# Product 3 of two feature tiles of gate and up computed in Strassen's form

## The chip, the cores and the metric

One Trainium2 chip; the program runs on one of its cores. The metric is the device time of one execution in microseconds. A core has TensorE (PE, matmuls, with its weight loads shown as PEld), VectorE (DVE), ScalarE (ACT), GpSimd (POOL) and SyncE (SP, which here issues the DMA transfers). Each engine works its own instructions in order; waits on semaphores join them.

## The reference

One inference step of a hybrid decoder layer with a model width of 1024, on 16 meta tokens, 1024 prompt tokens and 8 sample tokens, 1048 in all. The part that matters here is the feed-forward block, which stands before and after the mixer, with 2816 features:

```
def swiglu(x, wg, wu, wd):
    return (jax.nn.silu(x @ wg) * (x @ wu)) @ wd
...
h = h + 0.5 * swiglu(rmsnorm(h, n1), w1g, w1u, w1d)
...
h = h + 0.5 * swiglu(rmsnorm(h, n2), w2g, w2u, w2d)
```

Everything is float32. Here `x @ wg` and `x @ wu` are called gate and up.

## The kernel before

Features lie in 22 tiles of 128. For one tile, gate and up are computed together as a 2 x 2 block product: the left side has gate and up as its rows and the two halves of the 1024-long contraction (four K tiles of 128 each) as its columns; the right side has the two K halves as rows and two token parts as columns. A block of the right side exists for each of two token halves c; the token quarters are 262 wide in the first FFN and 258 in the second. The 2 x 2 product is done in Strassen's form (Winograd's variant), with seven products in place of eight, numbered 1 to 7, from sums of weight blocks (left) and sums of token blocks (right).

Float32 accuracy comes from splitting each operand into a high part (a float32r copy) and a low part (the difference), and three matmuls for each K tile: high with high, high with low, low with high (`mm3`, L163 to L165). So one product is 2 token halves x 4 K tiles x 3 = 24 matmuls and one tile is 7 x 24 = 168.

The products run in the order 1, 6, 2, 5, 7, 3, 4. Each writes a pair of PSUM banks ("acc", two pairs in rotation); 2 adds to the pair that 1 has filled, 3 to that of 5, and 4 to that of 7. When both token halves of a product are done, VectorE or ScalarE reads the pair (`post` in `pair`): ScalarE copies 1 (L574); VectorE adds 6 (L576), multiplies 2 by the norm's factor (L569) and ScalarE takes silu of it (L581), VectorE adds 5 (L583), 7 (L585), 3 (L587) and 4 (L593), and multiplies silu(gate) by up into the hidden tile (L608). All of TensorE, VectorE, ScalarE and SP is issued in an order written out by hand: `Steps` holds a list of half products (12 matmuls each, 14 for one feature tile), and every other job is put before the step with a given number.

For the left side (`Left`, from L465 on) the weights are loaded eleven steps before the tile's first product (L476, 256 KB each: gate and up, two K halves), the four sums stand seven to five steps before it on VectorE (L482), and the splits run just ahead of the products: ScalarE casts (L486), VectorE subtracts (L490). The right side's split operands are made once per FFN by `Blocks` and stay.

The hidden tiles of two feature tiles at a time go through `Hidden.jobs`: VectorE makes four differences (L734), and SP stores seven blocks to DRAM (L737), from where the down product loads them later. The slots that matter: 9 temporaries "t" of 524 columns, 8 raw weight tiles "r", 6 split weight tiles "ws", 8 slots "s" and 30 slots "u" of 1056 columns; in PSUM four banks "acc" and four banks "mis".

In the first FFN the first two feature tiles are done without Strassen's form (`Plain`); in the second FFN the first two go through `pair` in a special order. The other twenty tiles of each FFN go through `pair` one by one, with `Hidden.jobs` behind every two.

Of the kernel before, what the change touches and what calls it, by code (L numbers as in the profile page):

```python
# [9 lines left out]
F32 = mybir.dt.float32  # L10
# [326 lines left out]
class Blocks:  # L337
# [25 lines left out]
    def src(self, p):  # L363

        return self.b[7 if p == 12 else p]
# [74 lines left out]
class Steps:  # L440
# [9 lines left out]
    def add(self, mm, post=None):  # L450
        self.steps.append((mm, post))

    def run(self):
        for i, (mm, post) in enumerate(self.steps):
            for fn in self.at.pop(i, ()):
                fn()
            mm()
            if post:
                post()
        for i in sorted(self.at):  # L460
            for fn in self.at[i]:
                fn()


class Left:  # L465
# [27 lines left out]
        self.hi(p)  # L493
        self.lo(p)

    def plan(self, S, s0, late, sums):
        for ps, ds, fn in (
            ((1, 7, 4, 2), (-11, -11, -10, -10), self.load),
            ((5, 6, 7, 3), [d + sums for d in (-7, -7, -6, -5)], self.sum_),
            (ORDER, [2 * i - 4 + late for i in range(7)], self.hi),  # L500
            (ORDER, [2 * i - 3 + late for i in range(7)], self.lo),
        ):
            for p, d in zip(ps, ds):
                S.before(s0 + d, lambda p=p, fn=fn: fn(p))
# [195 lines left out]
            S.before(at + i, lambda fn=fn, n=n: fn(n))  # L700


FP = DFF // P // 2

DORDER = (1, 5, 6, 7, 3, 4, 2)
# [3 lines left out]
class Hidden:  # L709
# [3 lines left out]
        self.K = K  # L713
        self.d = {p: K.dram.tile([P, 2, FP, self.K.Q], F32, name=K.uid("hd")) for p in ORDER}

    def jobs(self, S, i, hid, e0, e1):

        K = self.K
        t, b = {}, {}

        def block(n):

            return hid[n // 2][0][:, n % 2 * 2 * self.K.Q : n % 2 * 2 * self.K.Q + 2 * self.K.Q]

        def val(p):
            return b[p] if p in b else block({1: 0, 12: 1, 2: 2, 3: 3}[p])

        def sub(p, x, y):
            s = {5: 0, 6: 0, 7: 1, 4: 1}[p]
            if s not in t:  # L730
                t[s] = K.slot("s", self.K.T)
            o = (p in (6, 4)) * 2 * self.K.Q
            b[p] = t[s][:, o : o + 2 * self.K.Q]
            K.nc.vector.tensor_sub(b[p], val(x), val(y))  # L734

        def store(p):
            K.nc.sync.dma_start(self.d[p][:, :, i, :], halves(val(p)))  # L737

        ks = (1, 3, 5) if i < FP - 1 else (1, 2, 3)
        for at, args in zip((e0 + 1, *(e1 + k for k in ks)), ((5, 12, 1), (6, 3, 5), (7, 3, 12), (4, 2, 6))):  # L740
            S.before(at, lambda args=args: sub(*args))
            S.before(at + 2, lambda p=args[0]: store(p))
        for at, p in ((e0 + 2, 1), (e1 + 1, 3), (e1 + 2, 2)):
            S.before(at, lambda p=p: store(p))

    def load(self, S, p, at):
# [148 lines left out]
def ffn(K, wg, wu, wd, ops, spread, src, first, after, late_r, plain=False):  # L895
# [10 lines left out]
    with K.tc.manual_schedule(engines={E.PE, E.DVE, E.Activation, E.SP}):  # L906
# [3 lines left out]
        if plain:  # L910
            hid = [[], []]
            lefts = [Left(K, [w[:, k : k + 4, f * P : f * P + P] for w, k in ((wgv, 0), (wuv, 0), (wuv, 4), (wgv, 4))], 4) for f in range(2)]
            first(S, *lefts)
            for f in range(2):
                p = Plain(K, lefts[f], ops, spread, hid[f], f == 1)
                p.add(S)
                p.late(S, late_r + 6 * f)
            hidden.jobs(S, 0, hid, late_r + 6, late_r + 12)
        for i in range(int(plain), NF // 2):
            hid, e = [], []  # L920
            for f in (2 * i, 2 * i + 1):
                hid.append([])
                pair(K, S, wgv, wuv, f, ops, spread, hid[-1], late_r, f == (2 if plain else 1), first if f == 0 else None)
                e.append(len(S.steps))
            hidden.jobs(S, i, hid, *([late_r + 6, max(late_r + 7, e[1])] if i == 0 else e))
# [1355 lines left out]
```

## Time and profile before

| | |
|---|---|
| runs | 1946.50, 1946.09, 1944.43 us; median 1946.09 |
| span of the profiled execution | 1943.5 us |
| PE busy | 99% |
| DVE busy | 74% |
| ACT busy | 42% |
| POOL busy | 5% |
| matmuls | 16,800 |
| DMA | 258 MB, 133 GB/s mean |

The page gives the span of one profiled execution, from its first to its last instruction, and beside it the busy share of each engine. Matmuls are pipelined: a row shows one as 0.28 to 0.29 us long, though the next one starts 0.12 us after it. So what TensorE does is read from the starts of its matmuls and from the waits in brackets, not from its busy share. A row of the timeline gives the start, the duration, the engine, the line, the operation, and in brackets how long the engine had been idle and what released it. The page gives no time around the span; the profiled execution stands 2.6 us under the median of the runs.

The steady part of gate and up lies at about 110 to 340 us (first FFN) and 1300 to 1620 us (second FFN).

### The profile page before, as it was taken

The page shows a single profiled execution, that of the slowest core. Times are in us where ns is not written, and L with a number is a line of the kernel's source. Part 1 is how long each engine was busy: PE and PEld are TensorE (multiplying, and loading weights), DVE is VectorE, ACT ScalarE, POOL GpSimd, SP SyncE. Part 2 cuts the span into 40 slices and gives each one's busy share as a digit, 9 for nine tenths or more (in the row PEclk, how much of TensorE's full clock was granted, in tenths as well). Part 3 has the DMA queues.
Part 4 walks back from the last instruction along what each step waited for, and adds up shares of the span by engine and source line. Part 5 has one row for each costly group of instructions (what it writes and reads, how often), then busy time and mean ns, then how long its engine had stood idle before and what let it go on. Part 6 is the DMA issues. An engine that isn't in the chain of part 4 may idle for free.

```text
span 1943.5 us, 41139 instructions
## 1 busy us (share of the span) xinstructions
PE 1921.7 (99%) x16800; PEld 1887.7 (97%) x16800; DVE 1434.7 (74%) x2516; ACT 823.6 (42%) x1558; POOL 90.3 (5%) x144
## 2 busy tenths in 40 slices
PE   9999999999999999999999999999999999999998
PEld 8999999999999999999899999999999999999998
DVE  7877777778688877576575556987777777768974
ACT  7522222224543644466564545742222222354343
POOL 3000000000000510000000002200000000000000
PEclk9999999999999999999999999999999999999999
DMA  8142332325977541221453254223332433487852
GB/s 246 47 129 83 101 114 83 114 85 157 289 230 257 172 146 53 64 88 48 117 160 93 79 176 137 91 80 99 94 104 82 124 90 100 153 257 231 280 182 86
DMA packets 324207, 258.45 MB, mean 133 GB/s; under 512 B 18923, under 2 KB 298731, under 8 KB 324011
## 3 DMA queue, kind: packets, MB, share of 16 engines
q1 hardware_dynamic: 323779, 255.79, 43.4%
q8 instruction: 132, 2.16, 0.4%
q14 instruction: 56, 0.46, 0.1%
q0 software_dynamic: 224, 0.04, 0.0%
q10 hardware_dynamic: 16, 0.00, 0.0%
HBM read 190.79 MB, written 65.05 MB: 132 GB/s over the span
## 4 chain that ended last, share of the span: by engine, by line
PE 93%; DVE 4%; issue 1%; ACT 1%; DMA 1%; SPq 0%; POOL 0%; DVEq 0%; ACTq 0%; POOLq 0%
PE acc L163 29%; PE acc L164 28%; PE acc L165 28%; PE mis L1677 1%; PE mis L1390 0%; DVE u L376 0%; PE mis L1739 0%; PE mis L1384 0%; DMA s<-in_x_prompt_dram 0%; DVE ws L490 0%; DVE t L321 0%; PE mis L1768 0%; PE mis L1377 0%; PE mis L1668 0%; PE mis L223 0%
## 5 line engine op out<-in xcount | busy, mean ns | idle before, releaser
L163 PE MATMUL acc<-u,ws 128*128 128x258 f32 (+3 forms) x4514 | 1316.4, 292 | 5.6 <-DVE t L583 2.3
L165 PE MATMUL acc<-u,ws 128*128 128x258 f32 (+3 forms) x4514 | 1304.0, 289 | 1.3 <-DVE ws L490 1.3
L164 PE MATMUL acc<-u,ws 128*128 128x258 f32 (+3 forms) x4514 | 1304.8, 289 | 0.2 <-DVE u L324 0.2
L163 PEld LDWEIGHTS acc<-u,ws 128*128 128x128 f32 x4514 | 852.6, 189 | 15.3 <-issue 10.0
L164 PEld LDWEIGHTS acc<-u,ws 128*128 128x128 f32 x4514 | 854.9, 189 | 1.4 <-DVE u L324 0.7
L165 PEld LDWEIGHTS acc<-u,ws 128*128 128x128 f32 x4514 | 852.2, 189 | 2.6 <-DVE ws L490 2.1
L490 DVE TENSOR_TENSOR ws<-r,ws 128x512 fp32r<-128x512 f32 x302 | 208.4, 691 | 69.6 <-ACT ws L486 69.5
L486 ACT CAST ws<-r 128x512 fp32r<-128x512 f32 x302 | 170.3, 614 | 4.8 <-DVE r L482 4.8
L602 ACT ACTIVATE t<-t 128x516 f32<-128x516 f32 (+1 forms) x43 | 27.4, 640 | 289.3 <-DVE t L569 289.3
L482 DVE TENSOR_TENSOR r<-r,r 128x512 f32<-128x512 f32 x168 | 115.7, 690 | 8.4 <-DMA r<-in_w_ffn_up_dram 6.8
L581 ACT ACTIVATE t<-t 128x516 f32<-128x516 f32 (+1 forms) x41 | 26.2, 639 | 197.2 <-DVE t L569 197.2
L762 DVE TENSOR_TENSOR u<-u,u 128x1048 fp32r<-128x1048 f32 (+3 forms) x84 | 97.2, 1158 | 9.8 <-ACT u L758 9.8
L250 POOL TENSOR_TENSOR t<-t,t 128x262 f32<-128x262 f32 (+1 forms) x56 | 58.2, 1048 | 783.2 <-DMA u<-hd 601.3
L158 DVE TENSOR_TENSOR ws<-r,ws 128x512 fp32r<-128x512 f32 x88 | 60.9, 700 | 40.6 <-ACT ws L157 40.1
L569 DVE TENSOR_TENSOR t<-t,u 128x516 f32<-128x516 f32 (+1 forms) x127 | 85.1, 697 | 2.8
L758 ACT CAST u<-u 128x1048 fp32r<-128x1048 f32 (+3 forms) x84 | 83.0, 988 | 4.0 <-DMA u<-hd 4.0
L820 ACT CAST ws<-u 128x512 fp32r<-128x512 f32 (+1 forms) x72 | 42.1, 585 | 98.9 <-DVE u L815 96.8
L825 DVE TENSOR_TENSOR ws<-r,ws 128x512 fp32r<-128x512 f32 (+1 forms) x84 | 56.3, 679 | 29.4 <-ACT ws L820 29.4
L849 DVE SCALAR_TENSOR_TENSOR s<-acc,s 128x524 f32<-128x524 f32 (+3 forms) x86 | 53.8, 649 | 32.8 <-PE acc L165 32.5
L820 ACT CAST ws<-r 128x512 fp32r<-128x512 f32 (+1 forms) x84 | 48.0, 582 | 65.1 <-DVE r L815 30.2
L574 ACT COPY t<-acc 128x516 f32<-128x516 f32 (+2 forms) x43 | 25.0, 582 | 103.5 <-PE acc L165 102.5
L569 DVE TENSOR_TENSOR t<-acc,u 128x516 f32<-128x516 f32 (+1 forms) x41 | 28.7, 699 | 49.5 <-PE acc L165 49.5
(420 smaller groups left out, 1844.8 us busy)
## 6 DMA issues: line engine op xcount, KB each, us to landing
r<-in_w_ffn_down_dram SPq DMA_DIRECT2D x128, 256.0 KB
hd<-s SPq DMA_DIRECT2D x93, 258.0 KB
r<-in_w_ffn_gate_dram SPq DMA_DIRECT2D x88, 256.0 KB
r<-in_w_ffn_up_dram SPq DMA_DIRECT2D x88, 256.0 KB
hd<-s SPq DMA_DIRECT2D x77, 262.0 KB
u<-hd SPq DMA_DIRECT2D x36, 516.0 KB
u<-hd SPq DMA_DIRECT2D x28, 524.0 KB
r<-in_w_in_dram SPq DMA_DIRECT2D x56, 256.0 KB
```

Source lines behind the costliest of these rows:

```text
L158: self.nc.vector.tensor_sub(lo, src, hi.bitcast(F32))
L163: mm(ps, whi, xhi, start=first, stop=False, skip_group_check=more)
L164: mm(ps, whi, xlo, start=False, stop=False, skip_group_check=more)
L165: mm(ps, wlo, xhi, start=False, stop=last, skip_group_check=more)
L250: K.nc.gpsimd.tensor_add(self.sq[q], self.sq[q], t)
L482: self.K.nc.vector.tensor_tensor(self.raw[p], self.raw[x], self.raw[y], op)
L486: self.K.nc.scalar.copy(self.w[p][:, : self.n * P], self.raw[p])
L490: self.K.nc.vector.tensor_sub(t[:, 512 : 512 + w], self.raw[p], t[:, :w].bitcast(F32))
L569: nc.vector.tensor_mul(t, t if src is None else src, spread.lanes(i, cs))
L758: K.nc.scalar.copy(hi, lo.bitcast(F32))
L762: K.nc.vector.tensor_sub(lo, lo.bitcast(F32), hi.bitcast(F32))
L820: nc.scalar.copy(w[p, j, g][:, : n * P], src)
```

## The change

In both FFNs, twenty of the feature tiles are taken two at a time (`two_pairs`, ten calls for each FFN). The two tiles still run products 1, 6, 2, 5, 7, 4 one after the other, each in 2 token halves: 12 steps for one tile in place of 14. Product 3 of the two tiles is taken out of them and done as one 2 x 2 block product of its own, again in Strassen's form: its rows are the two feature tiles, its contraction halves are two K tiles each, its columns are the two token quarters c. That is seven sub-products of 2 K tiles x 3 = 6 matmuls (`Third`). They run inside the second tile, one behind each of its steps 3 to 9 (`Steps.also`), in the order 1, 6, 2, 7, 5, 3, 4, into single banks "mis", 262 or 258 columns wide.

The left sums of the sub-products are made on VectorE from the raw weight sums of product 3 (`Third.sums`, four subtractions or additions 256 wide), and split by ScalarE and VectorE (`Third.hi`, `Third.lo`: three 512 wide, one 256 wide). Their results are combined by ScalarE (two copies) and VectorE (five additions 262 or 258 wide, `Third.post`) into a slot "s", and `second` adds them to the gate of the second token quarters of each tile (on VectorE, 524 or 516 wide; before, `post` of product 3 added its PSUM sum there). The right operands of the sub-products are sums of token blocks; `SubBlocks` makes them once for each FFN, behind the first two feature tiles: twelve VectorE instructions and four ScalarE casts 524 or 516 wide, kept in three slots "s" and one slot "u".

`Left` still loads the same weights eleven steps ahead and makes the same four sums. The seven stores of `Hidden.jobs` stay; that of block 1 is put nine steps earlier (`first=-7`).

```
--- before.py
+++ after.py
@@ -450,6 +450,11 @@
     def add(self, mm, post=None):
         self.steps.append((mm, post))
+    def also(self, fn):
+        mm, post = self.steps[-1]
+        self.steps[-1] = (mm, lambda: (post and post(), fn()))
     def run(self):
         for i, (mm, post) in enumerate(self.steps):
             for fn in self.at.pop(i, ()):
@@ -493,12 +498,12 @@
         self.hi(p)
         self.lo(p)
-    def plan(self, S, s0, late, sums):
+    def plan(self, S, s0, late, sums, order=ORDER):
         for ps, ds, fn in (
             ((1, 7, 4, 2), (-11, -11, -10, -10), self.load),
             ((5, 6, 7, 3), [d + sums for d in (-7, -7, -6, -5)], self.sum_),
-            (ORDER, [2 * i - 4 + late for i in range(7)], self.hi),
-            (ORDER, [2 * i - 3 + late for i in range(7)], self.lo),
+            (order, [2 * i - 4 + late for i in range(7)], self.hi),
+            (order, [2 * i - 3 + late for i in range(7)], self.lo),
         ):
             for p, d in zip(ps, ds):
                 S.before(s0 + d, lambda p=p, fn=fn: fn(p))
@@ -700,6 +705,232 @@
             S.before(at + i, lambda fn=fn, n=n: fn(n))
+ORDER2 = (1, 6, 2, 5, 7, 4)
+SUB = (1, 6, 2, 7, 5, 3, 4)
+class SubBlocks:
+    def __init__(self, K, ops):
+        self.K, self.ops = K, ops
+    def jobs(self, S, at):
+        K = self.K
+        nc = K.nc
+        b, hi, lo = {}, {}, {}
+        w = 2 * K.Q
+        def part(t, a):
+            return t[:, a * w : a * w + w]
+        def join(n, a, c):
+            b[n] = K.t(w)
+            h, l = self.ops[c].op[3]
+            nc.vector.tensor_add(b[n], part(h, a).bitcast(F32), part(l, a).bitcast(F32))
+        def sub(n, x, y):
+            nc.vector.tensor_sub(b[n], b[x], b[y])
+        def place(n):
+            s, i = {6: (0, 0), 7: (0, 1), 5: (1, 0), 4: (1, 1)}[n]
+            for d, tags in ((hi, "su"), (lo, "ss")):
+                if s not in d:
+                    d[s] = K.slot(tags[s], 2 * w, F32R)
+            self.op[n] = part(hi[s], i), part(lo[s], i)
+        names = {5: 11, 7: 12, 6: 22, 4: 21}
+        def cast(n):
+            place(n)
+            nc.scalar.copy(self.op[n][0], b[names[n]])
+        def low(n):
+            nc.vector.tensor_sub(self.op[n][1], b[names[n]], self.op[n][0].bitcast(F32))
+        self.op = {}
+        todo = [
+            [(join, 11, 0, 0), (join, 12, 0, 1)],
+            [(sub, 11, 12, 11), (join, 22, 1, 1)],
+            [(sub, 12, 22, 12), (sub, 22, 22, 11), (cast, 6)],
+            [(low, 6), (cast, 7), (join, 21, 1, 0)],
+            [(low, 7), (sub, 21, 21, 22), (cast, 5)],
+            [(low, 5), (cast, 4)],
+            [(low, 4)],
+        ]
+        for i, fns in enumerate(todo):
+            for fn, *args in fns:
+                S.before(at + i, lambda fn=fn, args=args: fn(*args))
+    def right(self, m):
+        if m in self.op:
+            return self.op[m]
+        a, c = {1: (0, 0), 2: (1, 0), 3: (1, 1)}[m]
+        w = 2 * self.K.Q
+        return tuple(t[:, a * w : a * w + w] for t in self.ops[c].op[3])
+class Third:
+    def __init__(self, K, lefts, sub):
+        self.K, self.lefts, self.sub = K, lefts, sub
+        self.w, self.ps = {}, {}
+    def plan(self, S, s1):
+        for d, fn, *args in (
+            (-2, self.sums, 0),
+            (-1, self.sums, 1),
+            (0, self.hi, 0),
+            (1, self.lo, 0),
+            (1, self.hi, 1),
+            (2, self.lo, 1),
+            (2, self.sums, 2),
+            (3, self.hi, 2),
+            (4, self.lo, 2),
+            (5, self.hi, 3),
+            (6, self.lo, 3),
+        ):
+            S.before(s1 + d, lambda fn=fn, args=args: fn(*args))
+    def sums(self, i):
+        x, y = (l.raw[3] for l in self.lefts)
+        sub, add = self.K.nc.vector.tensor_sub, self.K.nc.vector.tensor_add
+        h0, h1 = slice(0, 2 * P), slice(2 * P, 4 * P)
+        if i == 0:
+            self.r = self.K.raw()
+            sub(self.r[:, h0], x[:, h0], y[:, h0])
+            add(y[:, h0], y[:, h0], y[:, h1])
+        elif i == 1:
+            sub(self.r[:, h1], y[:, h0], x[:, h0])
+        else:
+            sub(x[:, h1], x[:, h1], self.r[:, h1])
+    def src(self, i):
+        x, y = (l.raw[3] for l in self.lefts)
+        return {0: x, 1: self.r, 2: y, 3: x[:, 2 * P :]}[i]
+    def hi(self, i):
+        src = self.src(i)
+        self.w[i] = self.K.ws()
+        self.K.nc.scalar.copy(self.w[i][:, : src.shape[1]], src)
+    def lo(self, i):
+        src, t = self.src(i), self.w[i]
+        w = src.shape[1]
+        self.K.nc.vector.tensor_sub(t[:, 512 : 512 + w], src, t[:, :w].bitcast(F32))
+    def mm(self, m):
+        K = self.K
+        t, o = {1: (0, 0), 2: (0, 256), 7: (1, 0), 6: (1, 256), 5: (2, 0), 4: (2, 256), 3: (3, 0)}[m]
+        b = {2: 1, 3: 5, 4: 7}.get(m, m)
+        if b not in self.ps:
+            self.ps[b] = K.psm()[:, : K.Q]
+        x = self.sub.right(m)
+        for k in range(2):
+            ks = slice(k * K.Q, k * K.Q + K.Q)
+            wh, wl = (self.w[t][:, d + o + k * P : d + o + k * P + P] for d in (0, 512))
+            K.mm3(self.ps[b], wh, wl, x[0][:, ks], x[1][:, ks], m == b and k == 0, k == 1, m != b)
+    def post(self, m):
+        K = self.K
+        nc, ps = K.nc, self.ps
+        if m == 1:
+            self.v = halves(K.t(2 * K.Q))
+            nc.scalar.copy(self.v[:, 0], ps[1])
+        elif m == 6:
+            nc.vector.tensor_add(self.v[:, 0], ps[6], self.v[:, 0])
+        elif m == 2:
+            q = K.slot("s", 4 * K.Q)
+            self.q = [halves(q[:, f * 2 * K.Q : f * 2 * K.Q + 2 * K.Q]) for f in range(2)]
+            nc.scalar.copy(self.q[0][:, 0], ps[1])
+        elif m == 5:
+            nc.vector.tensor_add(self.v[:, 1], ps[5], self.v[:, 0])
+            nc.vector.tensor_add(self.q[1][:, 1], ps[7], self.v[:, 1])
+        elif m == 3:
+            nc.vector.tensor_add(self.q[0][:, 1], ps[5], self.v[:, 0])
+        elif m == 4:
+            nc.vector.tensor_add(self.q[1][:, 0], ps[7], self.v[:, 0])
+def two_pairs(K, S, wg, wu, i, ops, spread, hids, sub, tight):
+    nc = K.nc
+    cs = slice(0, 2)
+    s0 = len(S.steps)
+    s1 = s0 + 2 * len(ORDER2)
+    tm = [{}, {}]
+    lefts = []
+    for n in range(2):
+        fs = slice((2 * i + n) * P, (2 * i + n) * P + P)
+        lefts.append(Left(K, [wg[:, 0:4, fs], wu[:, 0:4, fs], wu[:, 4:8, fs], wg[:, 4:8, fs]], 4))
+        lefts[n].plan(S, (s0, s1)[n], int(tight and n == 0), (3, 2)[n] * int(tight), ORDER2)
+    third = Third(K, lefts, sub)
+    third.plan(S, s1)
+    def temp(f, n):
+        if n not in tm[f]:
+            tm[f][n] = halves(K.t(2 * K.Q))
+        return tm[f][n]
+    def gate(f, n, t, src):
+        nc.vector.tensor_mul(t, src, spread.lanes(n, cs))
+        nc.scalar.activation(t, t, AF.Silu)
+    def out(f, n, u):
+        nc.vector.tensor_mul(u, u, spread.lanes(n, cs))
+        if not hids[f]:
+            hids[f].append(K.slot("s", K.T))
+        nc.vector.tensor_mul(halves(hids[f][0][:, n * 2 * K.Q : n * 2 * K.Q + 2 * K.Q]), temp(f, f"g{n}"), u)
+    def post(f, p, b):
+        if p == 1:
+            nc.scalar.copy(temp(f, "v"), b)
+        elif p == 6:
+            nc.vector.tensor_add(temp(f, "v"), b, temp(f, "v"))
+        elif p == 2:
+            gate(f, 0, temp(f, "g0"), b)
+        elif p == 5:
+            nc.vector.tensor_add(temp(f, "g1"), b, temp(f, "v"))
+        elif p == 7:
+            nc.vector.tensor_add(temp(f, "u1"), b, temp(f, "g1"))
+        elif p == 4:
+            u = temp(f, "v")
+            nc.vector.tensor_add(u, b, u)
+            out(f, 0, u)
+    def second(f):
+        g = temp(f, "g1")
+        nc.vector.tensor_add(g, g, third.q[f])
+        gate(f, 1, g, g)
+    def third_step(m):
+        third.mm(m)
+        third.post(m)
+    for f in range(2):
+        unit = Unit(K, lefts[f].w, [o.op for o in ops], 4, lambda p, cs, b, f=f: post(f, p, b))
+        for p in ORDER2:
+            for c in range(2):
+                j = len(S.steps) - s1
+                unit.step(S, p, c, (0, 1))
+                if 3 <= j < 10:
+                    S.also(lambda m=SUB[j - 3]: third_step(m))
+    S.before(s1 + 9, lambda: second(0))
+    S.before(s1 + 10, lambda: out(0, 1, temp(0, "u1")))
+    S.before(s1 + 11, lambda: second(1))
+    S.before(s1 + 12, lambda: out(1, 1, temp(1, "u1")))
+    return s1 + 10, s1 + 12, -7
 FP = DFF // P // 2
 DORDER = (1, 5, 6, 7, 3, 4, 2)
@@ -713,7 +944,7 @@
         self.K = K
         self.d = {p: K.dram.tile([P, 2, FP, self.K.Q], F32, name=K.uid("hd")) for p in ORDER}
-    def jobs(self, S, i, hid, e0, e1):
+    def jobs(self, S, i, hid, e0, e1, first=2):
         K = self.K
         t, b = {}, {}
@@ -740,7 +971,7 @@
         for at, args in zip((e0 + 1, *(e1 + k for k in ks)), ((5, 12, 1), (6, 3, 5), (7, 3, 12), (4, 2, 6))):
             S.before(at, lambda args=args: sub(*args))
             S.before(at + 2, lambda p=args[0]: store(p))
-        for at, p in ((e0 + 2, 1), (e1 + 1, 3), (e1 + 2, 2)):
+        for at, p in ((e0 + first, 1), (e1 + 1, 3), (e1 + 2, 2)):
             S.before(at, lambda p=p: store(p))
     def load(self, S, p, at):
@@ -916,8 +1147,14 @@
                 p.add(S)
                 p.late(S, late_r + 6 * f)
             hidden.jobs(S, 0, hid, late_r + 6, late_r + 12)
+        sub = SubBlocks(K, ops)
+        sub.jobs(S, late_r + (9 if plain else 14))
         for i in range(int(plain), NF // 2):
             hid, e = [], []
+            if i > 0:
+                hid = [[], []]
+                hidden.jobs(S, i, hid, *two_pairs(K, S, wgv, wuv, i, ops, spread, hid, sub, plain and i == 1))
+                continue
             for f in (2 * i, 2 * i + 1):
                 hid.append([])
                 pair(K, S, wgv, wuv, f, ops, spread, hid[-1], late_r, f == (2 if plain else 1), first if f == 0 else None)
```

## The prediction

> **What bounds the kernel now.** First the shares of the span by engine, then the windows of the two gate and up stages, which the change touches, and last single waits. Columns of a window row: microseconds, then busy time and instructions (x) of PE, its weight loads, DVE, ACT and POOL, then the granted clock.
>
> ```profile
> PE 1921.7 (99%) x16800; PEld 1887.7 (97%) x16800; DVE 1434.7 (74%) x2516; ACT 823.6 (42%) x1558; POOL 90.3 (5%) x144
> ...
> PE 93%; DVE 4%; issue 1%; ACT 1%; DMA 1%; SPq 0%; POOL 0%; DVEq 0%; ACTq 0%; POOLq 0%
> ```
>
> ```profile
> 78.00:99.00 21.00, 20.25 (x164) 19.83 (x163) 20.81 (x34) 6.78 (x12) 0.00 (x0) 1.00 0.24 81
> 200.00:250.00 50.00, 50.00 (x413) 50.00 (x413) 37.72 (x59) 13.20 (x24) 0.00 (x0) 1.00 0.43 122
> 1350.00:1400.00 50.00, 50.00 (x419) 50.00 (x419) 37.54 (x59) 13.15 (x24) 0.00 (x0) 1.00 0.37 107
> ```
>
> TensorE carries the chain. In the steady stage it starts a matmul every 0.121 us (50 us / 413) in the first FFN and 0.119 us (50 / 419) in the second, at full clock, and never waits. VectorE is busy three quarters of that time, ACT one quarter. So a matmul taken out is worth its 0.12 us, and any wait given to TensorE costs its whole length.
>
> **What the change removes.** Each pair of feature tiles had 2 x 7 products of 2 token halves, 4 K tiles and 3 matmuls: 336. Product 3 of both tiles (48 matmuls) becomes seven sub-products of 2 K halves x 3 = 42. That is 6 fewer, over ten pairs in each of two FFNs: 120 matmuls, 60 x 0.121 + 60 x 0.119 = 14.4 us gained.
>
> **What it adds on VectorE and ScalarE.** Per pair of tiles: weight splits go from two 512-wide ones to three and a half, four 256-wide sums are new, and five 262-wide reads of sub-products. In instructions of VectorE, one wide and ten half-wide ones more; of ScalarE, four more. How close they follow each other:
>
> ```profile
> 209.91 0.69 DVE L585 TENSOR_TENSOR t<-acc,t 128x524 f32<-128x524 f32 x1
> 210.52 0.68 DVE L490 TENSOR_TENSOR ws<-r,ws 128x512 fp32r<-128x512 f32 x1
> 212.18 0.70 DVE L587 TENSOR_TENSOR t<-acc,t 128x524 f32<-128x524 f32 x1 [0.98 <-PE acc L165]
> 212.92 0.70 DVE L569 TENSOR_TENSOR t<-t,u 128x524 f32<-128x524 f32 x1
> ...
> 703.31 0.42 DVE L324 TENSOR_TENSOR u<-t,u 128x262 fp32r<-128x262 f32 x1
> 703.65 0.42 DVE L849 SCALAR_TENSOR_TENSOR s<-acc,s 128x262 f32<-128x262 f32 x1
> ```
>
> Wide and independent: 0.61 us from start to start; wide and dependent on the one before: 0.74; half-wide: 0.34, and 0.47 when the next depends on it (0.43 and the 0.04 between 212.88 and 212.92). So VectorE gains 0.61 + 10 x 0.34 = 4.0 us of work per pair, on 0.754 x 40.7 = 30.7 us (37.72 / 50 of 336 x 0.121): 34.7 of 39.9 us. ScalarE at 26% hides its four. The average has room; what matters is the order in which the queue is served.
>
> The Trainium skill, "VectorE: DVE Perf Modes", section "The TRN2 errata", gives a fp32 tensor_tensor (N+151)/0.96 ns and says many small tiles pay the fixed part each: 0.42 us for 256 columns, 4.9 us added by an estimate from that page. The duration agrees with the 0.42 of the row at 703.31, but the spacing there is 0.34, so by the trace the added work is 4.0; the page would add 0.9 us per pair to the queue, 18 us over twenty pairs if nothing hid it.
>
> **New wait 1: product 4 right behind product 7.** The order was 1, 6, 2, 5, 7, 3, 4 and becomes 1, 6, 2, 5, 7, 4. Products 7 and 4 share an accumulator pair: VectorE must read 7's sum before the first matmul of 4 adds to it, and in the built program that matmul does wait for that read. Product 3's 24 matmuls (2.9 us) used to lie between and covered it. Now nothing does in the first tile of a pair, and in the second only one sub-product (6 x 0.121 = 0.73 us). What such a read takes, and what a restart costs:
>
> ```profile
> 211.86 0.28 PE L165 MATMUL acc<-u,ws 128*128 128x262 f32 x1
> 211.98 0.28 PE L163 MATMUL acc<-u,ws 128*128 128x262 f32 x1
> ...
> 105.97 0.69 DVE L583 TENSOR_TENSOR t<-acc,t 128x524 f32<-128x524 f32 x1
> 106.59 0.68 DVE L482 TENSOR_TENSOR r<-r,r 128x512 f32<-128x512 f32 x1
> 106.79 0.19 PEld L163 LDWEIGHTS acc<-u,ws 128*128 128x128 f32 x1 [1.72 <-issue]
> 106.82 0.36 PE L163 MATMUL acc<-u,ws 128*128 128x262 f32 x1 [1.55 <-DVE t L583]
> 106.89 0.19 PEld L164 LDWEIGHTS acc<-u,ws 128*128 128x128 f32 x1
> 107.01 0.28 PE L164 MATMUL acc<-u,ws 128*128 128x262 f32 x1
> ```
>
> The last matmul of a product starts at 211.86, its reader at 212.18: 0.32. The read takes 0.70, TensorE starts 0.16 after it (106.66 to 106.82), and the second matmul follows after 0.19 in place of 0.12: 0.07. Without a wait the next matmul starts 0.12 after the last. First tile: 0.32 + 0.70 + 0.16 + 0.07 - 0.12 = 1.13 us per pair, with VectorE free at that moment.
>
> In the second tile the read stands behind other work. Zero is the start of the last matmul of sub-product 3, in the middle of product 7. VectorE: 0.32 the half-wide add of that sub-product; 0.79 `second(0)` adds it to the gate; 1.53 multiplies by the norm; 2.14 a low part of the next tile's weights; 2.76 the read of 7, to 3.46. TensorE may go on at 3.62, and would have at 19 x 0.121 = 2.30. Wait: 1.32 + 0.07 = 1.39 us. Bounds: 0.40 (1.13 - 0.73, VectorE free) and 2.0 (one more wide instruction ahead). I take 1.39, since all five instructions are in the queue in that order.
>
> **New wait 2: the weights of the tile after.** A pair now has 24 steps in place of 28, so the next loads stand two steps behind the last hidden products and no longer four. On SP's queue they are now right behind the store of block 3, which waits for the last hidden product of the second tile. The walk goes on: after the read of 7 at 2.76 come a half-wide add (3.38), then multiply, product, add, multiply, a difference for Hidden, a low part (3.72, 4.46, 5.07, 5.81, 6.42, 7.03), the read of 4 (7.63), multiply 8.37, product 9.10, multiply 9.72, product 10.45 to 11.15. Only then may SP issue. Its spacing and the landing:
>
> ```profile
> 238.71 1.86 SPq L737 DMA_DIRECT2D hd<-s  x3
> 240.65 0.57 SPq L476 DMA_DIRECT2D r<-in_w_ffn_gate_dram  x1
> 241.32 1.19 SPq L476 DMA_DIRECT2D r<-in_w_ffn_up_dram  x2
> ```
>
> ```profile
> 99.20 0.12 SPq L737
> ...
> 99.83 4.69 DMA r<-in_w_ffn_up_dram
> ...
> 104.64 0.70 DVE r L482
> ...
> 105.97 0.71 DVE t L583
> 106.68 0.14 issue
> 106.82 0.36 PE acc L163
> ```
>
> About 0.64 us each: store 11.2, gate load 11.85, up load 12.5, another store 13.1, second up load 13.8. The chain rows show the mechanism once in the kernel before: a store held SP to 99.2, the up load behind it took 4.69 us, the weight sum came late, a PSUM read behind it came late, TensorE stood. With 4.69 the second up load lands at 18.5. VectorE would have come to the sum at 15.5 (seven wide instructions after 10.45, two of them dependent). Now: sum 18.5, second sum 19.2, gate read of product 2 from 19.85 to 20.55, TensorE at 20.7. TensorE ran product 4 from 3.62, starts the next tile at 6.6 and wants product 7, in the bank of product 2, at 6.6 + 96 x 0.121 = 18.2. Wait: 2.5 + 0.07, say 2.5 us, and the queue is then about 0.3 us late for wait 1 of that tile. It occurs between pairs: 18 times. Bounds: 0, if a load needs 2.2 us or less, and 3.1 with 5.3 us (issue at 283.2, sum at 288.64 below).
>
> ```profile
> 282.55 1.29 SPq L476 DMA_DIRECT2D r<-in_w_ffn_up_dram  x2
> ...
> 288.64 1.42 DVE L482 TENSOR_TENSOR r<-r,r 128x512 f32<-128x512 f32 x2 [0.86 <-DMA r<-in_w_ffn_up_dram]
> ```
>
> I take 2.5, from 4.69, the only landing on the chain. The other loads of a pair (first steps of its second tile) need 5.3 us of lead at most and have about that.
>
> **Set-up and moves.** `SubBlocks` adds once per FFN twelve wide instructions, 12 x 0.61 = 7.4 us of VectorE, and four casts on ScalarE that are hidden. In the first FFN they come where VectorE has no idle time (20.81 of 21.00 us at 78 to 99), so nearly all shows, 7 us; in the second a quarter of the time is idle, 3 us. Sum 10, bounds 0 and 18. The store of hidden block 1 goes nine steps earlier, where SP is idle: nothing. Loads and stores are as many as before. Three of eight "s" slots are held for the stage; the stores that free the rest end some steps before the new hidden tile wants them: nothing, up to 0.5 us per pair if they are late.
>
> **The sum.** Per pair: waits 1.13 + 1.39 = 2.52, twenty times 50.4. Late weights 18 x (2.5 + 0.3) = 50.4. Set-up 10. Less 14.4. Together +96 us on a span of 1943.5, whose runs have a median of 1946.09, 2.6 above: 2042 us.
>
> **The rivals.**
> *The loads come in time.* Then only the bank wait stays: 50.4 + 10 - 14.4 = +46, 1992 us. For it: in the steady stage before, eleven weight sums waited 0.2 us together (last number of the row, 200 to 250 us). Against it: the second up load was issued 4 to 5 us ahead of its sum then, and would be 1.7 ahead now, behind a store that VectorE releases late. Chance 0.25, from 1975 to 2010.
>
> ```profile
> L482 DVE TENSOR_TENSOR r<-r,r 128x512 f32<-128x512 f32 x11 | 7.6, 687 | 0.2
> ```
>
> *The reads cost TensorE nothing, and the change saves its matmuls.* Decides if both waits at product 4 together stay under 0.72 us per pair. Then 1946 - 14.4 = 1932. The place is the start of product 4; nothing but the 0.73 us of one sub-product lies there, so even with VectorE free they are 1.13 + 0.40. Chance 0.05.
> *The clock drops after the longer waits.* In this trace it stays 1.00 through the 1.55 us wait at 106.82. If each of the 18 long waits were followed by one product (24 matmuls, 2.9 us) at half clock, 18 x 2.9 = 52 more: 2094. Chance 0.06. The Trainium skill, "TensorE: Matmul & The Clock Gate", section "Why this matters for your kernels", warns of idle gaps above about 3 us; these are below it, so by that rule it should not happen.
>
> **How the numbers follow.** The forecast, bank waits and late weights, has 0.62, from 2012 to 2062 (late weights 1.2 to 3.1 us, set-up 0 to 18). Loads in time 0.25, the saving 0.05, the clock 0.06, no change by 0.2% either way (about what this kernel's runs can tell) 0.02. The range 1978 to 2062 takes in the forecast and nearly all of the loads in time, and leaves some 0.15 outside. Faster 0.05, same 0.02, slower 0.93.
>
> **What the profile after would show.** Waits of TensorE on the read of product 7, forty, of about 1.1 and 1.4 us in turn. Waits of TensorE on the gate read some 18 times, and VectorE's sums on an up load. Some 120 matmuls fewer, clock 1.00, ScalarE never the releaser. VectorE's busy time up by about 90 us (20 x 4.0 + 2 x 7.4 = 95, less what overlaps). I am wrong if TensorE starts product 4 without a gap, or if the sums find their weights there.

## The result and the profile after

The changed kernel takes 2070.92 us (median of five runs, 2064.86 to 2072.99) against 1946.09 us beside it: the ratio is 1.0637, 95% interval 1.0623 to 1.0651. The forecast was 2042, its range ended at 2062. The direction and the two waits were right; some 25 us came from a case that was given 0.06.

The page of the changed kernel, busy shares and chain of waits by engine:

```profile
PE 1948.1 (94%) x16680; PEld 1901.6 (92%) x16680; DVE 1537.7 (74%) x2760; ACT 862.3 (42%) x1646; POOL 85.2 (4%) x144
...
PE 71%; DVE 18%; DMA 5%; issue 2%; SPq 2%; ACT 1%; DVEq 0%; POOL 0%; ACTq 0%; POOLq 0%
```

TensorE's share fell from 99% to 94%, and VectorE and the transfers took 23% of the chain (5% before). VectorE was 103 us busier, where about 90 had been expected. The matmuls are 120 fewer, as counted.

What TensorE waited for, the two greatest of the list of waits (total us, times, longest), and below it who waited for the weights on VectorE:

```profile
PE acc L163 <- DVE t L904: 48.8, 40, 3.7
PE acc L163 <- DVE t L885: 45.2, 19, 4.4
...
DVE r L487 <- DMA r<-in_w_ffn_up_dram: 56.8, 18, 5.1
```

L904 is the read of product 7, L885 the gate read of product 2, L487 the sum that wants the second up load. These are the two waits of the forecast, in their predicted number: forty, and one in each of the eighteen places between two pairs (the nineteenth is 0.32 us at 1380.11, inside a pair). Fourteen of the eighteen are 2.0 to 2.4 us long and four are 3.0 to 4.4. The same walk through the queues at one pair, timeline rows of VectorE, SP and TensorE:

```profile
254.28 0.28 PE L165 MATMUL mis<-u,ws 128*128 128x262 f32 x1
...
256.46 0.28 PE L165 MATMUL mis<-u,ws 128*128 128x262 f32 x1
257.87 0.36 PE L163 MATMUL acc<-u,ws 128*128 128x262 f32 x1 [1.13 <-DVE t L904]
258.07 0.28 PE L164 MATMUL acc<-u,ws 128*128 128x262 f32 x1
...
274.83 0.36 PE L163 MATMUL acc<-u,ws 128*128 128x262 f32 x1 [2.00 <-DVE t L885]
279.29 0.36 PE L163 MATMUL acc<-u,ws 128*128 128x262 f32 x1 [1.31 <-DVE t L904]
```

```profile
254.60 0.43 DVE L855 TENSOR_TENSOR s<-mis,t 128x262 f32<-128x262 f32 x1 [1.30 <-PE mis L165]
255.06 0.70 DVE L912 TENSOR_TENSOR t<-t,s 128x524 f32<-128x524 f32 x1
255.80 0.70 DVE L885 TENSOR_TENSOR t<-t,u 128x524 f32<-128x524 f32 x1
256.42 0.69 DVE L495 TENSOR_TENSOR ws<-r,ws 128x512 fp32r<-128x512 f32 x1
257.02 0.70 DVE L904 TENSOR_TENSOR t<-acc,t 128x524 f32<-128x524 f32 x1
...
264.86 0.70 DVE L892 TENSOR_TENSOR s<-t,t 128x524 f32<-128x524 f32 x1
...
272.65 1.42 DVE L487 TENSOR_TENSOR r<-r,r 128x512 f32<-128x512 f32 x2 [2.70 <-DMA r<-in_w_ffn_up_dram]
```

```profile
261.48 4.62 SPq L968 DMA_DIRECT2D hd<-s  x2
266.20 0.56 SPq L481 DMA_DIRECT2D r<-in_w_ffn_gate_dram  x1
266.85 0.50 SPq L481 DMA_DIRECT2D r<-in_w_ffn_up_dram  x1
267.40 0.52 SPq L968 DMA_DIRECT2D hd<-s  x1
268.01 0.56 SPq L481 DMA_DIRECT2D r<-in_w_ffn_up_dram  x1
```

Zero of the walk is 254.28. The read of 7 starts at 2.74 (walk 2.76), the last hidden product ends at 11.28 (11.15), the second up load is issued at 13.73 (13.8) and the sum that wants it starts at 18.37 (18.5). TensorE starts product 4 at 3.59 (3.62). The queues did what the order of issue said.

The bracket of a wait is shorter than its cost. At 257.87 it says 1.13; without a wait the matmul of 258.07 would have stood at 256.46 + 2 x 0.12 = 256.70, so the cost is 1.37: 0.24 more. At the 2.19 us wait that ends at 136.22 it is 0.24 as well. Over 59 waits this adds 14 us to the list's 48.8 + 45.2.

What the forecast did not have is in the granted clock:

```profile
core 0: 2069.2 us, clock 0.985
```

```profile
core 0: 1943.5 us, clock 0.997
```

A mean of 0.985 over 2069.2 us is 31.0 us lost to a lower clock (the kernel before, second fence: 5.8). The clock has three places, so such a loss is good to about 1 us. The five runs of the changed kernel differ by about as much as this loss does:

| span, us | mean clock | span x clock |
|---|---|---|
| 2063.1 | 0.988 | 2038.3 |
| 2066.7 | 0.987 | 2039.8 |
| 2069.2 | 0.985 | 2038.2 |
| 2071.1 | 0.984 | 2038.0 |
| 2071.3 | 0.984 | 2038.2 |

Windows of the changed kernel, around four waits of the same kind (columns as in the prediction; the last but two is the clock):

```profile
133.27:136.68 3.41, 1.22 (x11) 1.04 (x10) 2.60 (x4) 0.57 (x2) 0.00 (x0) 1.00 0.79 254
136.68:140.09 3.41, 3.41 (x18) 3.41 (x17) 2.59 (x4) 2.66 (x6) 0.00 (x0) 0.50 0.00 0
181.05:184.47 3.42, 1.73 (x14) 1.76 (x15) 2.77 (x5) 1.84 (x4) 0.00 (x0) 1.00 0.48 151
184.47:187.88 3.41, 2.11 (x17) 1.92 (x16) 3.34 (x8) 1.39 (x3) 0.00 (x0) 1.00 0.01 2
225.43:228.84 3.41, 1.20 (x10) 1.02 (x9) 2.60 (x4) 0.61 (x2) 0.00 (x0) 1.00 0.79 259
228.84:232.25 3.41, 3.41 (x18) 3.41 (x18) 2.60 (x4) 2.62 (x6) 0.00 (x0) 0.50 0.00 0
273.22:276.63 3.41, 1.80 (x15) 1.83 (x16) 2.72 (x6) 1.92 (x4) 0.00 (x0) 1.00 0.46 143
276.63:280.04 3.41, 2.10 (x18) 1.93 (x17) 3.38 (x7) 1.32 (x3) 0.00 (x0) 1.00 0.01 2
```

All four are late-weight waits of about 2.0 to 2.2 us. Two are followed by 3.41 us at a clock of 0.50, two are not. The half-clock stretches begin on one grid: 136.68, 228.84, 416.57, 508.73, 1375.72 and the others lie whole multiples of 3.4133 us apart. Where a wait falls into one stretch of this grid, TensorE is idle for 2.2 of 3.41 us and the next stretch runs at half clock (1.71 us lost by the clock); where the edge cuts these waits, each side has under 1.7 us of idle time and nothing happens. Seventeen half-clock stretches were found in all, 17 x 1.71 = 29 us; the other 2 us lie at the end of the program. Twelve of the seventeen stand behind ten of the eighteen late-weight waits, 20 us. Of the other five, one stands at the start of the program, three in the first pairs of the two FFNs, and one behind a wait of 2.13 us in the last pair of all.

What such a stretch costs in the end is less than its 1.71 us:

```profile
136.22 0.36 PE L163 MATMUL acc<-u,ws 128*128 128x262 f32 x1 [2.19 <-DVE t L885]
...
141.78 0.36 PE L163 MATMUL acc<-u,ws 128*128 128x262 f32 x1 [0.89 <-DVE t L904]
```

From one restart to the next it is 5.56 us here, and 4.46 at 274.83 to 279.29 above, where the clock stayed up: 1.10 us more. TensorE itself loses 1.10 + 0.42 = 1.52, but VectorE goes on at its own pace meanwhile, and the next wait is 0.42 us shorter (0.89 in place of 1.31). The list's 48.8 holds these shorter waits already.

By the measured terms the difference of the spans comes out as 48.8 + 45.2 + 14.2 (waits) - 14.4 (matmuls) + 6.5 (set-up, below) + 25.2 (clock) = 125.5; it is 2069.2 - 1943.5 = 125.7. That it closes to 0.2 is luck: each term is good to a few us.

### The profile page after: what moved, and what is told of

Its sections match the earlier page's. It is cut to its first block, busy times and chain, and to the rows that moved or that the text cites. A ratio compares the mean times of both kernels' runs of the same rounds, so it can differ in the third digit from the quotient of the medians.

```text
span 2069.2 us, 41308 instructions
## 1 busy us (share of the span) xinstructions
PE 1948.1 (94%) x16680; PEld 1901.6 (92%) x16680; DVE 1537.7 (74%) x2760; ACT 862.3 (42%) x1646; POOL 85.2 (4%) x144
## 4 chain that ended last, share of the span: by engine, by line
PE 71%; DVE 18%; DMA 5%; issue 2%; SPq 2%; ACT 1%; DVEq 0%; POOL 0%; ACTq 0%; POOLq 0%
PE acc L163 20%; PE acc L165 20%; PE acc L164 20%; DMA r<-in_w_ffn_up_dram 4%; DVE s L892 2%; DVE r L487 2%; DVE ws L495 2%; DVE t L885 2%; DVE t L889 2%; PE mis L163 2%; PE mis L165 1%; PE mis L164 1%; DVE t L904 1%; DVE t L912 1%; SPq L481 1%
## 5 line engine op out<-in xcount | busy, mean ns | idle before, releaser
L163 PE MATMUL acc<-u,ws 128*128 128x258 f32 (+4 forms) x4194 | 1241.1, 296 | 98.8 <-DVE t L904 48.8
L165 PE MATMUL acc<-u,ws 128*128 128x258 f32 (+4 forms) x4194 | 1226.4, 292 | 1.6 <-DVE ws L495 1.6
L164 PE MATMUL acc<-u,ws 128*128 128x258 f32 (+4 forms) x4194 | 1224.4, 292 | 0.2 <-DVE u L324 0.2
L163 PEld LDWEIGHTS acc<-u,ws 128*128 128x128 f32 x4194 | 802.2, 191 | 119.0 <-issue 85.6
L164 PEld LDWEIGHTS acc<-u,ws 128*128 128x128 f32 x4194 | 805.3, 192 | 1.4 <-DVE u L324 0.6
L165 PEld LDWEIGHTS acc<-u,ws 128*128 128x128 f32 x4194 | 802.9, 191 | 3.8 <-DVE ws L495 2.2
L886 ACT ACTIVATE t<-t 128x524 f32<-128x524 f32 (+1 forms) x80 | 51.1, 639 | 370.2 <-DVE t L885 370.2
L495 DVE TENSOR_TENSOR ws<-r,ws 128x512 fp32r<-128x512 f32 x262 | 180.8, 691 | 25.3 <-ACT ws L491 25.2
L487 DVE TENSOR_TENSOR r<-r,r 128x512 f32<-128x512 f32 x168 | 115.8, 691 | 58.9 <-DMA r<-in_w_ffn_up_dram 56.8
L491 ACT CAST ws<-r 128x512 fp32r<-128x512 f32 x262 | 151.8, 616 | 4.8 <-DVE r L487 4.8
L820 ACT CAST ws<-r 128x512 fp32r<-128x512 f32 x80 | 45.3, 566 | 119.1 <-DVE r L809 69.5
L158 DVE TENSOR_TENSOR ws<-r,ws 128x512 fp32r<-128x512 f32 x88 | 60.9, 700 | 39.9 <-ACT ws L157 37.4
L989 ACT CAST u<-u 128x1048 fp32r<-128x1048 f32 (+3 forms) x84 | 82.8, 987 | 5.3 <-DMA u<-hd 5.2
L163 PE MATMUL mis<-u,ws 128*128 128x258 f32 (+1 forms) x238 | 67.9, 285 | 3.5 <-DVE t L852 2.7
L896 ACT COPY t<-acc 128x524 f32<-128x524 f32 (+1 forms) x40 | 23.8, 595 | 110.5 <-PE acc L165 109.5
L165 PE MATMUL mis<-u,ws 128*128 128x258 f32 (+1 forms) x238 | 67.3, 283 | 1.0 <-DVE ws L825 1.0
```

The source lines that it names most:

```text
L158: self.nc.vector.tensor_sub(lo, src, hi.bitcast(F32))
L163: mm(ps, whi, xhi, start=first, stop=False, skip_group_check=more)
L164: mm(ps, whi, xlo, start=False, stop=False, skip_group_check=more)
L165: mm(ps, wlo, xhi, start=False, stop=last, skip_group_check=more)
L487: self.K.nc.vector.tensor_tensor(self.raw[p], self.raw[x], self.raw[y], op)
L491: self.K.nc.scalar.copy(self.w[p][:, : self.n * P], self.raw[p])
```

## The experiments

Every ratio is to the kernel before, run beside it. "Lost" is (1 - mean clock) x span of the profiled run, good to about 1 us.

| kernel | median, us | ratio, 95% interval | lost, us |
|---|---|---|---|
| the change | 2070.92 | 1.0637 (1.0623 to 1.0651) | 31.0 |
| e1: product 7 before 5 | 2056.86 | 1.0570 (1.0550 to 1.0590) | 26.8 |
| e2: stores later | 2001.24 | 1.0287 (1.0270 to 1.0304) | 10.0 |
| e3: both | 1991.47 | 1.0236 (1.0221 to 1.0251) | 12.0 |
| e4: long wait filled | 2060.09 | 1.0588 (1.0558 to 1.0619) | 12.3 |
| e5: e3, differences on GpSimd | 2012.59 | 1.0330 (1.0316 to 1.0344) | 12.1 |
| e6: no set-up | 2064.40 | 1.0604 (1.0587 to 1.0621) | 33.1 |
| e7: e5, later start | 2003.18 | 1.0284 (1.0270 to 1.0298) | 8.0 |
| e8: a third of the long wait filled | 2066.20 | 1.0606 (1.0590 to 1.0622) | 20.6 |
| e9: e8, short wait filled as well | 2067.82 | 1.0610 (1.0588 to 1.0631) | 20.7 |

### e2: the late weights alone

The stores of hidden blocks 3 and 2, which held SP's queue, go two steps later, behind the loads, in every pair but the last of each FFN.

```
-        for at, p in ((e0 + first, 1), (e1 + 1, 3), (e1 + 2, 2)):
+        for at, p in ((e0 + first, 1), (e1 + 1 + late, 3), (e1 + 2 + late, 2)):
```

> Edit: the stores of hidden blocks 3 and 2 are put two steps later, behind the next tile's weight loads on SP's queue. Theory: the loads come in time, the waits on the gate read (45 us) go, and with no wait above 1.4 us left the clock stays at 1.00 and gives back some 22 us: about 2003 us. Rival (the clock loss has another cause than the long waits): 45 us alone, about 2026 us, clock mean still 0.985.

2001.24 us, 70 us less than the change; 2003 had been expected. In the list of TensorE's waits, the gate read L885 is gone from the top, and VectorE no longer waits for up loads:

```profile
PE acc L163 <- DVE t L904: 44.3, 39, 3.7
PE mis L163 <- DVE t L852: 4.0, 3, 1.9
```

Of the 70 us, the wait with its restarts was 45.2 + 19 x 0.24 = 49.8, and 21 are clock: span times clock fell from 2038.2 to 1999.2 x 0.995 = 1989.2, 49.0. So the mechanism behind "New wait 2" is shown: a store that VectorE releases late, ahead of a load in SP's queue. It cost the more of the two kinds of wait: of those that come back in every pair it alone was long enough to halve the clock.

### e1 and e3: the bank wait

Product 7 goes ahead of 5, so that the partner of 4 is read one product earlier.

```
-ORDER2 = (1, 6, 2, 5, 7, 4)
+ORDER2 = (1, 6, 2, 7, 5, 4)
...
+            nc.vector.tensor_add(temp(f, "u1"), b, temp(f, "u1"))
...
-            nc.vector.tensor_add(temp(f, "u1"), b, temp(f, "g1"))
+            nc.vector.tensor_add(temp(f, "u1"), b, temp(f, "v"))
```

The first line with "u1" is one wide VectorE instruction more for each tile, at the read of 5: the sum of 7 no longer finds 5 in it.

> Edit: product 7 goes ahead of 5 (1, 6, 2, 7, 5, 4), so that 24 matmuls of 5 lie between 7 and 4; VectorE pays one more wide addition per tile. Theory (TensorE loses 49 us to the reads of 7, 45 us to late weights, and about 26 us to the halved clock after the longer waits): the waits at product 4 go, but the weight loads hang on VectorE's queue and not on TensorE, so what the second tile of a pair saves (1.2 us) comes back at the next gate read, now about 3.6 us. Only the first tile's 1.1 us per pair is kept: about 2045 us, clock loss as large or larger. Rival (the waits are independent): all 49 us come back, 2020 us.

> Edit: both of the above together. Theory: no wait of TensorE in the steady stage, clock 1.00, only the set-up in the first pair of each FFN remains (about 10 us) against 14.4 us fewer matmuls: 1942 to 1948 us. Rival (VectorE's queue, about 90% busy, takes over as the bound): new waits of half a us or more in every pair, 1960 us or above.

e1 gave 2056.86, neither the 2045 of the theory nor the rival's 2020; e3 gave 1991.47 against the theory's 1942 to 1948. In both the read of 7 is gone from the waits, but others stand there. The list of e1, then that of e3:

```profile
PE acc L163 <- DVE t L885: 49.0, 19, 4.7
PE acc L163 <- DVE t L908: 18.2, 19, 2.9
PE acc L165 <- DVE ws L495: 15.6, 23, 1.0
```

```profile
PE acc L163 <- DVE t L908: 18.2, 19, 2.9
PE acc L165 <- DVE ws L495: 15.5, 22, 1.0
```

L908 is now the read of product 4 (the expectation of e5 below calls it the second read of 5), whose pair of banks product 6 of the next tile wants, and L495 a low part of the weights: both late because VectorE's queue is. In e1 these lists add up to 82.8 us against the change's 94.0, which with 4 us less lost to the clock is about the gain of 14. A window of e3 over one pair, and one inside it:

```profile
209.01:251.26 42.25, 40.68 (x331) 40.28 (x330) 36.47 (x62) 12.71 (x25) 0.00 (x0) 1.00 0.31 95
243.30:263.30 20.00, 18.43 (x150) 18.03 (x149) 18.90 (x31) 6.02 (x11) 0.00 (x0) 1.00 0.44 134
```

VectorE is busy 36.47 of 42.25 us over the pair (86%), and 18.90 of 20.00 where the waits lie: the end of one pair and the beginning of the next, with the products of both token quarters, four differences, and the low parts of the next tile. That is what remains when both waits are taken out. Of e3's 1992.8 x 0.994 - 1943.5 x 0.997 = 43 us, the two waits with restarts are 18.2 + 15.5 + 41 x 0.24 = 43.5, the set-up 6.5, the matmuls -14.4; some 7 are smaller waits.

### e5 and e7: VectorE's queue relieved

e5 is e3 with the four differences of `Hidden.jobs` on GpSimd and their stores later; e7 is e5 with the first of the ten pairs done as before, and the set-up spread over three times the steps.

```
-            K.nc.vector.tensor_sub(b[p], val(x), val(y))
+            (K.nc.gpsimd if late else K.nc.vector).tensor_sub(b[p], val(x), val(y))
```

```
-            if i > 0:
+            if i > 1:
...
-                S.before(at + i, lambda fn=fn, args=args: fn(*args))
+                S.before(at + 3 * i, lambda fn=fn, args=args: fn(*args))
```

> Edit: as the run with both repairs, and the four differences of each hidden pair (but the last pair's) go from VectorE to GpSimd, their stores two steps later. Theory (what is left, 18 us of waits on the second read of 5 and 15 us on low parts of weights, is VectorE's queue, full from the last sub-products to the next tile's sums): 2.4 us less work per pair in that stretch takes most of both away: about 1958 us. Rival (GpSimd is too slow or holds VectorE up): 1985 us or above.

> Edit: as the run with GpSimd, and the second pair of tiles of each FFN still runs product by product as before, while SubBlocks is spread over three times as many steps; so nine pairs per FFN are changed. Theory (waits and set-up gone, clock full): 13 us fewer matmuls less a few us of leftover waits, 1936 to 1944 us, below the kernel before. Rival (VectorE's queue still fills in the second tile): 1955 us or above.

e5 was slower than e3 by 21 us, e7 slower than e3 by 12 (18 and 9 by their ratios); both times lie where the rivals had put them. The timeline of e5 shows why taking instructions from VectorE did not help it:

```profile
207.85 1.65 POOL L966 TENSOR_TENSOR s<-s 128x524 f32<-128x524 f32 x1 [31.63 <-DMA r<-in_w_ffn_up_dram]
208.37 1.70 DVE L885 TENSOR_TENSOR t<-t,u 128x524 f32<-128x524 f32 x1
```

The multiply at L885 takes 0.70 us in every row of the changed kernel shown above, and 1.70 beside a difference on GpSimd. It starts 0.52 after GpSimd's instruction and ends 0.57 after it. So it lost 1.00 us, more than the 0.61 (the spacing of wide instructions in the prediction) that the difference takes on VectorE itself. In e5's trace each of the 72 differences on GpSimd overlaps an instruction of VectorE that is 0.5 to 1.1 us longer than elsewhere. These are 67 us in all, against 72 x 0.61 = 44 taken off. The Trainium skill, "SBUF — State Buffer", section "Who interferes with whom", says that a VectorE instruction with two SBUF inputs contends with a GpSimd instruction that reads SBUF; these rows agree. e7, against e5, shows only that the early start and the set-up, with one changed pair fewer in each FFN, were together worth some 9 us.

### e6: without the set-up

`SubBlocks` is left out, and four of the sub-products take plain token blocks in place of their sums, so the result is another.

```
-        a, c = {1: (0, 0), 2: (1, 0), 3: (1, 1)}[m]
+        a, c = {1: (0, 0), 2: (1, 0), 3: (1, 1), 4: (1, 1), 5: (1, 0), 6: (0, 0), 7: (0, 1)}[m]
...
-        sub.jobs(S, late_r + (9 if plain else 14))
```

> Edit: the changed kernel with the work of SubBlocks left out; the sub-products read unsummed token blocks in its place, so the result is another. Prices the set-up. By the prediction's term it is 10 us: 2061 us. Rival (the waits in the first pair also cost clock windows): 15 to 20 us, 2051 to 2056 us.

2064.40: the set-up is worth 2070.92 - 2064.40 = 6.5 us (10 had been taken, bounds 0 and 18). By the two intervals this is good to about 4 us: the clock adds noise of its own to a difference this small.

### e4, e8 and e9: waits filled with matmuls

The clock is the term that needed a test. Matmuls whose result nobody reads are put where TensorE waits, ahead of product 7 of the first tile: e4 has seventeen (about the whole wait), e8 six (0.73 us of it), e9 six there and six ahead of product 4.

```
+    def junk():
+        ps = K.psm()[:, : K.Q]
+        for _ in range(17):
+            nc.tensor.matmul(ps, lefts[0].w[5][:, :P], ops[0].op[5][0][:, : K.Q], start=True, stop=True)
...
+                if i > 1 and (f, p, c) == (0, 7, 0):
+                    S.before(len(S.steps), junk)
```

> Edit: the changed kernel with 17 more matmuls (2.06 us) into an unused bank ahead of product 7 of the first tile of each pair from the second pair on; their result is not used. They fill the wait for the gate read. Theory (idle TensorE halves the clock): the time falls though work is added, by about 20 us to 2050 us, clock mean 0.995 or above. Rival (the clock loss is not tied to the wait): the clock stays near 0.985 and the time at 2071 us or a few us above.

> Six matmuls whose result nobody reads (0.73 us) stand ahead of product 7 of the first tile of a pair, in eighteen pairs. They are shorter than the wait of about 2.2 us that lies there, so TensorE goes on at the same moment as before, but stands still for about 1.5 us and no longer 2.2. Theory (the clock is halved for 3.41 us after a stretch of a 3.41 us grid in which TensorE was idle for more than about 1.85 us): the wait on the gate read falls to about 45 - 18 x 0.73 = 32 us in the list, most half-clock stretches go (lost to the clock under 10 us, 29 in the changed kernel), and the time falls to 2045 to 2055 us although work was added. Rival (the clock goes with the number of waits, or with their place behind a late load): the same loss of 25 to 30 us and 2065 to 2075 us.

> As the run with six matmuls ahead of product 7, and six more ahead of product 4 of the first tile, where TensorE waits 1.13 us. Theory: the two waits of the first tile lie about 4.5 us apart, a stretch of 3.41 us can hold parts of both; with the second one down to 0.4 us still fewer stretches reach 1.85 us of idle time. Lost to the clock under 8 us, time 2040 to 2052 us, and no more than 3 us above the run with one filling. Rival: the filling itself costs its 0.73 us (the read of product 7 comes no later than TensorE), and the time rises by up to 18 x 0.73 = 13 us over the run with one filling.

e4 took 2060.09, 11 us less than the change (2050 had been expected), although it does 306 matmuls more and delivers the same. The waits of e4 and of e8:

```profile
PE acc L163 <- DVE t L904: 52.1, 40, 3.7
PE acc L163 <- DVE t L885: 4.7, 7, 1.9
```

```profile
PE acc L163 <- DVE t L904: 49.8, 40, 3.7
PE acc L163 <- DVE t L885: 32.5, 19, 2.6
```

In e4 the loss to the clock fell from 31.0 to 12.3 us, and one half-clock stretch is left behind a late-weight wait, of twelve. The span of the profiled run fell by 17.4 us (2069.2 to 2051.8). The other three runs of e4 were slower, with span times clock up to 2056 against 2038, and no trace shows why.

In e8 the wait fell to 32.5 us as worked out (32), and the loss to 20.6. The expected "under 10" was missed, and the time, 2066.20, lies where the rival had put it and not at 2045 to 2055. Stretches of 3.41 us counted in the traces say why. About 10 to 12 us of the loss hang on waits that the edits leave alone (the first and the last pairs of the FFNs, the end of the program), as the 12.3 left in e4 shows. And the filling was too short: ten stretches of e8 with 1.75 us of idle time and more were each followed by a half-clock one, and six more lie at 1.70 to 1.74, just under. The rival's cause is not borne out even so: the late-weight waits are as many as before and in the same places, but five of the eighteen were followed by half clock, against ten in the changed kernel, and each of the five has 1.75 us or more in one stretch.

In e9 the second filling cost 1.6 us over e8, within the 3 us of the theory. It gained nothing on the clock, and 2067.82 missed the expected 2040 to 2052.

What follows: idle time of TensorE sets the clock (work added in the wait gives time back), and it counts by stretch. All eleven traces were cut into the stretches of each run's own grid, some 6,520. The 83 with 1.88 us of idle time and more were each followed by one at half clock; from 1.73 to 1.88 six of twenty were. Under 1.73 nineteen of some 6,420 were: nine that ran at half clock themselves (0.65 us of idle time held it there), two near 102 us (1.64 in the changed kernel, 1.60 in e9), two in the last 11 us of a program, and six without any idle time, of which the next section shows one.

No version tried beats the kernel before.

## Why the prediction was wrong

- *What bounds the kernel*: right. TensorE carried the chain, and each wait given to it cost its whole length and a little more.
- *Matmuls removed*: 120, as counted.
- *New wait 1*: right. Predicted were 1.13 and 1.39 us in turn, 50.4 in all, the first 0.3 later behind late weights. Measured with the restart are 1.31 + 0.24 = 1.55 and 1.13 + 0.24 = 1.37; in all 48.8 + 40 x 0.24 = 58.4, against 55.8 with the 18 x 0.3. Without late weights, in e2, the first wait reads 0.89 (at 222.6), which with the restart is the predicted 1.13; so late weights add 0.42 and not 0.3.
- *New wait 2*: right. 18 x 2.5 = 45 predicted, 45.2 + 19 x 0.24 = 49.8 measured. The landing taken from one row (4.69) held at the pair shown: the load issued at 268.01 was there at 272.65. The four waits of 3.0 us and more show that it is not the same everywhere: the sum before the longest of them (4.43 us, at 322.64) started at 320.47, 7.1 us after the issue of its load. The rival "the loads come in time", 0.25, did not occur; e2 made it occur, and gave 2001 where 1992 had been worked out.
- *Set-up*: 6.5, good to about 4, in place of 10.
- *The sum*: +96 forecast; without the clock, span times clock rose from 1943.5 x 0.997 = 1937.7 to 2038.2, +100.5.
- *The clock*: this step failed. The sum has no term for it: the rival "The clock drops after the longer waits" got 0.06, and "clock 1.00" stood among the signs. The loss to the clock was 31.0 us, 25 more than before. 20 us of it stand behind ten of the eighteen late-weight waits, not the 52 of the rival: a half-clock stretch is 3.41 us, and only a wait that falls into one stretch brings it. So the time lies between forecast and rival.

The reason against the rival was one row, the 1.55 us wait at 106.82 with a clock of 1.00. 1.55 lies under the 1.73 to 1.88 us at which the clock falls, the forecast's waits of about 2.3 us were over it, and between them the row says nothing. The trace of before did hold a row that speaks for the rival, in windows that the prediction did not look at, in the stage between the two feed-forward blocks, with the timeline of TensorE below:

```profile
752.38:755.79 3.41, 3.41 (x28) 3.11 (x28) 1.91 (x5) 2.50 (x3) 0.00 (x0) 1.00 0.51 129
755.79:759.20 3.41, 3.41 (x12) 3.41 (x13) 3.28 (x13) 0.27 (x1) 0.00 (x0) 0.50 0.65 169
```

```profile
752.23 1.28 PE L1263 MATMUL mis<-sel,u 16*128 16x8 f32 x10
...
754.77 0.96 PE L1263 MATMUL mis<-sel,u 16*128 16x8 f32 x8
```

The clock halved there after a stretch without idle time, filled for some 2.1 us with matmuls that are eight columns wide. The columns call these busy; by the clock it looks as if they count as idle. No run here changed them, but all eleven traces have the 24 of them. In six of them so many lie in one stretch that 1.74 to 1.98 us of it are without any other matmul, and half clock followed in all six. In the other five an edge of the grid divides the group, 1.40 us at most are without another matmul, and it never followed. A clock that falls with no wait at all should have moved the chance of that rival well above 0.06.

The Trainium skill was given too much weight at this place. The Trainium skill, "TensorE: Matmul & The Clock Gate", section "What's actually happening", states a free-running window of 3413 ns; the grid of 3.4133 us agrees. The rule of the Trainium skill that the prediction cites, gaps above about 3 us, does not: 2.2 us in one stretch were enough.

## What to carry to other kernels

A wait that is new on TensorE costs its length, 0.24 us of restart, and, if it can fill more than half of a 3.41 us stretch, up to 1.71 us more each time that it falls so (1.10 where a shorter next wait gives some back): price waits of 1.8 us and above with that term, by the share of grid phases in which they fit into one stretch (ten of eighteen here). Before a stage is shortened in steps, walk the in-order queue of SP: a store whose data come late holds every load behind it, and here moving two stores was worth 70 us. Where VectorE is near full for 20 us at a time, room in its average (86% busy in e3) does not help, and GpSimd made none here (e5).

## What the runs showed of the hardware

- The granted clock fell to 0.50 for one stretch of 3.41 us, on a grid of 3.4133 us that runs through the whole program and starts at another phase in each run. Idle time of 1.88 us and more within one stretch was always followed by it, under 1.73 us seldom (the counts stand with e4, e8 and e9). The same kernel differs by 8 us from run to run (2063.1 to 2071.3), about as much as its loss to the clock does.
- At half clock VectorE catches up: where a half-clock stretch follows a late-weight wait, the next wait on L904 was 0.89 us (at 141.78 and 233.90 in the changed kernel), elsewhere 1.31, so a part of each stretch's loss comes back.
- A group of 24 matmuls eight columns wide, busy by the profile, was followed by half clock as idle time would be (1.74 to 1.98 us of them in one stretch, in six of eleven traces; 1.40 us at most in the other five, and no half clock).
- A VectorE instruction of 0.70 us took 1.70 beside a GpSimd instruction of 1.65 that began 0.52 us before it.
